# Early products of an output projection one block later, its late heads ahead of the last transposes, and two blocks' splits held behind evacuations

## The chip, the cores and the metric

The kernel runs on one core of a Trainium2 chip. The metric is the device time of one execution in microseconds. The core has a matrix engine (TensorE, PE in the profile), a vector engine (VectorE, DVE), a scalar engine (ScalarE, ACT), GpSimd (POOL) and SyncE (SP), whose queue issues most of the DMA transfers. Each engine takes its instructions in the order in which they stand for it, and waits on semaphores for the others.

## The reference, cut to what matters

Two layers over 1024 tokens of width 1024. The first mixes tokens by latent attention, the second by differential attention; each mixer and each feed-forward is followed by a normalisation of the sum with its input. The change lies at the end of the second layer's mixer:

```python
def block(args):                       # one block of 128 queries
    logits = einsum('bqhmd,bkhmd->bmhqk', q_b, k) * scale - slopes * dist   # two maps m per head
    logits = where(chunk_mask, logits, NEG_BIG)
    p = softmax(logits)
    a = p[:, 0] - lam * p[:, 1]
    return einsum('bhqk,bkhe->bqhe', a, v)
...
o = _rmsnorm(o, g_sub) * (1.0 - lambda_init)     # per head
mix = o.reshape(b, s, 8 * 128) @ w_o
h = _layernorm(ALPHA * h + mix, ...)
h = _layernorm(ALPHA * h + (silu(gate) * up) @ w_down, ...)
```

There are 8 heads of width 128 and 8 blocks of 128 queries; block i sees keys 0 to 128 (i + 1).

## The kernel before

All products are kept to float32 accuracy by splitting each operand into a high and a low part in float32r: ScalarE casts the high part, VectorE (or GpSimd) subtracts it for the low one, and three products, high by high, high by low and low by high, are added in PSUM.

**Attention of the second layer.** `attention` goes through the 64 pairs of head and block, head by head; the last head takes its blocks in the order 6, 7, 4, 5, 2, 3, 0, 1. For each pair there are three steps. `score` (two pairs ahead) makes the scores of both maps in PSUM, VectorE adds the bias and takes the maximum (L231), ScalarE exponentiates and sums (L234), VectorE takes the reciprocal (L236), GpSimd scales the second map (L1306) and VectorE joins the two (L1307). `turn` transposes the probabilities on TensorE into PSUM (L160, tiles `pt`), and ScalarE (L255, `pth`) and VectorE (L256, `ptl`) evacuate their high and low parts. `mix`, once for two blocks, multiplies them by the values (L267, tile `o`), and VectorE copies the result into `bo` (L1316). Per head the rows are then normalised: squares on ScalarE (L1331), a sum over partitions on TensorE (L1337, `ms`), logarithm and exponential on ScalarE (L1340, L1342), and a product on GpSimd (L1343). Heads 0 to 5 are stored to DRAM; heads 6 and 7 stay in `bo`.

**Output projection.** `OutProj` loads its weights, already split, by SP's queue as soon as the input activations are no longer needed (L358, tiles `wo`; `who` and `wlo` for heads 6 and 7, L363), and reads back heads 0 to 5 of a query block (`of`, L371). The table in the caller puts its steps in between the last head's pairs: after pair `b + slot` (b = 54) `early` multiplies some of heads 0 to 5 of the first block (6) or the second (7); `late` splits heads 6 and 7 of a block, multiplies them and adds the result to the residual (L414, with a sum for the normalisation). `rest` then does the remaining blocks whole, 4, 5, 2, 3, 0, 1: `of` loads and splits heads 0 to 5 (L394 on ScalarE, L395 on VectorE), `late` the other two, and `layer_norm` (L178 to L196) and `raw_x` (transposes `xTp`) follow. After it comes the feed-forward.

**What sets the order.** The program is written in this order, but the framework reorders it: it lays the instructions on a modelled timeline, by when their operands are ready there and by their priority, and each engine's list comes out of that. `high_priority` raises a step; `behind(i, j)` keeps instruction i after j. The PSUM banks in this stage are 3 for scores and sums (`s`), 2 for `m`, 2 for transposes (`t`) and 1 for `o`. `newest["hi"]` and `newest["lo"]` name the last `pth` and `ptl` evacuations written so far.

## Time and profile before

| | |
|---|---|
| time, median of 3 runs | 2294.41 us (2293.27 to 2299.95) |
| profiled execution, its own time | 2294.99 us |
| its span in the trace | 2293.2 us, mean TensorE clock 0.996 |
| busy: PE, DVE, ACT, POOL | 2251.4, 1560.4, 1018.6, 877.9 us |
| last head of the attention with the early products | about 1500 to 1564 us |
| rest of the output projection | about 1564 to 1640 us |
| second feed-forward | from 1640 us to the end |

The rows of the trace quoted below name an engine, a line, an operation and a tile. In rows of the timeline the first number is the start in microseconds from the beginning of the span, the second the duration; brackets give the idle time just before, and what ended it. A mean of TensorE's granted clock stands in each window's row, 1.00 being full. Matmuls are pipelined: their durations overlap, so their cost on a full engine is the distance between starts.

### The profile page before, as it was taken

To read this page: it belongs to the slowest core of one execution; us is meant where nothing else is said; L and a number is where in the kernel's file an instruction comes from. 1 tells how busy PE (TensorE), PEld (TensorE's weight loads), DVE (VectorE), ACT (ScalarE), POOL (GpSimd) and SP (SyncE) were. 2 spreads that over 40 slices of the span, in tenths; PEclk is the share of its full clock that TensorE was granted. 3 is DMA by queue.
4 is the path that set the end of the run, shared out by engine and by line. 5 is a ranking of instruction groups with operands and counts; after the bars stand their busy time and mean duration, and the time that the engine had idled before them with its cause. 6 is when DMAs were issued, how large, how long until landed. Compare 5 with 4: busy or idle time off the path is not lost. (4 is left out here: it accounts for less than half of the span.)

```text
span 2293.2 us, 31159 instructions
## 1 busy us (share of the span) xinstructions
PE 2251.4 (98%) x11426; PEld 1918.7 (84%) x11426; DVE 1560.4 (68%) x2887; ACT 1018.6 (44%) x2101; POOL 877.9 (38%) x682
## 2 busy tenths in 40 slices
PE   9999999999999999999999999999999999999997
PEld 9888998888888887888888898977778888887886
DVE  6666665596656558777476766676587566658877
ACT  4465664342332324345455655555442233324353
POOL 2233451124444445555332424211024444436564
PEclk9999999999999999999999999999999999999999
DMA  5121335334323237544311202143344232337453
GB/s 205 41 94 61 117 99 190 142 139 144 108 87 120 93 116 305 200 176 166 104 45 33 69 25 70 38 193 120 124 166 155 70 128 80 127 126 301 144 203 123
DMA packets 104281, 289.33 MB, mean 126 GB/s; under 512 B 8640, under 2 KB 31808, under 8 KB 93632
## 3 DMA queue, kind: packets, MB, share of 16 engines
q1 hardware_dynamic: 100128, 277.90, 34.5%
q0 software_dynamic: 4000, 9.44, 1.4%
q8 instruction: 90, 1.47, 0.3%
q14 instruction: 63, 0.52, 0.1%
HBM read 205.78 MB, written 77.33 MB: 123 GB/s over the span
## 5 line engine op out<-in xcount | busy, mean ns | idle before, releaser
L486 ACT CAST op_g<-gr 128x512 fp32r<-128x512 f32 x240 | 147.5, 622 | 410.8 <-PE gb L531 229.9
L487 POOL TENSOR_TENSOR op_g<-gr,op_g 128x512 fp32r<-128x512 f32 x104 | 145.3, 1402 | 304.1 <-DVE tmp L622 154.0
L487 DVE TENSOR_TENSOR op_h<-rh,op_h 128x512 fp32r<-128x512 f32 x154 | 166.4, 1112 | 68.1 <-ACT op_h L486 68.1
L531 PE MATMUL ga<-xh_m,op_g 128*128 128x512 f32 x512 | 168.1, 389 | 0.0
L486 ACT CAST op_h<-rh 128x512 fp32r<-128x512 f32 x154 | 92.6, 619 | 148.7 <-DMA rh<-h_dr 39.9
L799 PE MATMUL dw<-op_w_t,op_h 128*128 128x512 f32 x660 | 151.5, 390 | 0.3 <-DVE op_h L487 0.3
L799 PEld LDWEIGHTS dw<-op_w_t,op_h 128*128 128x128 f32 x660 | 123.5, 188 | 26.4 <-DVE op_h L487 1.0
L234 ACT ACTIVATE l_b<-l_b,mx_b 128x256 f32<-128x256 f32 (+7 forms) x128 | 99.5, 778 | 75.9 <-DVE mx_b L231 74.0
L1306 POOL TENSOR_SCALAR l_b<-l_b,r_b,cst 128x128 f32<-128x128 f32 (+3 forms) x64 | 52.5, 821 | 207.6 <-DVE r_b L236 201.6
L487 POOL TENSOR_TENSOR op_w_t<-tt,op_w_t 128x512 fp32r<-128x512 f32 x66 | 100.1, 1521 | 80.0 <-ACT op_w_t L486 77.6
L799 PE MATMUL dx<-op_w_b,op_h 128*128 128x512 f32 x528 | 123.5, 394 | 5.4 <-ACT op_w_b L486 3.9
L799 PEld LDWEIGHTS dx<-op_w_b,op_h 128*128 128x128 f32 x528 | 99.8, 190 | 28.7 <-ACT op_w_b L486 4.7
L531 PE MATMUL gb<-t4h_f,op_g 128*128 128x512 f32 x352 | 115.9, 390 | 3.0 <-DVE tmp L614 3.0
L531 PE MATMUL gc<-b22h_f,op_g 128*128 128x512 f32 x352 | 115.6, 389 | 2.3 <-ACT op_g L486 2.3
L531 PE MATMUL gc<-t1h_f,op_g 128*128 128x512 f32 x352 | 115.5, 389 | 0.0
L487 DVE TENSOR_TENSOR op_g<-gr,op_g 128x512 fp32r<-128x512 f32 x136 | 109.5, 806 | 8.8 <-ACT op_g L486 8.2
L531 PE MATMUL gb<-t3h_f,op_g 128*128 128x512 f32 x352 | 115.2, 389 | 0.0
L531 PE MATMUL gb<-t2h_f,op_g 128*128 128x512 f32 x352 | 114.9, 389 | 0.0
L531 PEld LDWEIGHTS ga<-xh_m,op_g 128*128 128x128 f32 x512 | 96.1, 188 | 19.9
L487 POOL TENSOR_TENSOR op_g<-s,op_g 128x512 fp32r<-128x512 f32 x40 | 55.5, 1387 | 144.0 <-ACT op_g L486 144.0
L155 PE MATMUL bp<-xT_f,h_wb 128*128 128x512 f32 x256 | 102.8, 402 | 0.0
L157 PE MATMUL bp<-xT_f,l_wb 128*128 128x512 f32 x256 | 101.6, 397 | 0.0
(373 smaller groups left out, 6767.7 us busy)
## 6 DMA issues: line engine op xcount, KB each, us to landing
gr<-in_w_gu SPq DMA_DIRECT2D x44, 1024.0 KB, 6.8
rh<-h_dr SPq DMA_DIRECT2D x28, 1024.0 KB, 5.2
h_dr<-sh SPq DMA_DIRECT2D x22, 1024.0 KB, 4.9
h_dr<-hp SPq DMA_DIRECT2D x22, 768.0 KB, 4.1
tt<-in_w_dn SPq DMA_DIRECT2D x22, 512.0 KB, 7.6
rh<-h_dr SPq DMA_DIRECT2D x14, 768.0 KB, 4.4
z<-xs_dr SPq DMA_DIRECT2D x16, 512.0 KB, 11.1
rw_b<-in_w_dn SPq DMA_DIRECT2D x8, 1024.0 KB, 8.2
```

The costliest lines, as they stand in the source:

```text
L155: T.matmul(ps_out, lh, rh, start=(i == 0), stop=False)
L157: T.matmul(ps_out, ll, rh, start=False, stop=(i == n - 1))
L234: newest["exp"] = A.activation(l[:, :n], l[:, :n], AF.Exp, bias=mx, scale=-1.0, accum_out=sm).ins
L486: A.copy(hi, src)
L487: eng.tensor_tensor(lo, src, f32(hi), ALU.subtract)
L531: T.matmul(o, w[:, a, kc], x[b][:, k, :], start=(first and k == 0 and (a, b) == (0, 0)), stop=(k == 3 and a == 1), skip_group_check=True,)
L799: T.matmul(o, h[:, a, c], w[:, b_], start=(first and (a, b_) == (0, 0)), stop=(last and a == 1), skip_group_check=True,)
L1306: G.tensor_scalar(l1[:, :n], l1[:, :n], r1, nlam, ALU.mult, ALU.mult)
```

## The change

Three things are edited. The five `early` steps of the table move by one slot, so each is written one pair later; the `late` step of block 6 moves from slot 9 to slot 8, so it is written ahead of the transposes of the last pair instead of behind them; and in `split`, for blocks 4 and 5 and for the piece that begins at head 0, both halves are kept behind the newest `pth` and `ptl` evacuations, which at that point are the last ones of the attention.

```diff
         def split(self, tb, hs, o):
             oh, ol = (t[:, hs] for t in self.oh[tb])
-            A.activation(oh, o, AF.Copy, scale=self.scale)
-            V.scalar_tensor_tensor(ol, o, self.scale, f32(oh), ALU.mult, ALU.subtract)
+            i = A.activation(oh, o, AF.Copy, scale=self.scale)
+            j = V.scalar_tensor_tensor(ol, o, self.scale, f32(oh), ALU.mult, ALU.subtract)
+            if tb in LAST_ORDER[2:4] and hs.start == 0:
+                behind(i.ins, newest["hi"])
+                behind(j.ins, newest["lo"])
...
         for slot, what, args in (
-            (2, "early", (first, (0, 1))), (3, "early", (first, (2, 3))), (4, "early", (first, (4, 5))),
-            (6, "early", (second, (0, 1, 2))), (7, "early", (second, (3, 4, 5))),
-            (9, "late", (first,)),
+            (3, "early", (first, (0, 1))), (4, "early", (first, (2, 3))), (5, "early", (first, (4, 5))),
+            (7, "early", (second, (0, 1, 2))), (8, "early", (second, (3, 4, 5))),
+            (8, "late", (first,)),
         ):
```

Lines behind the edit stand three further down in the changed kernel (L406 becomes L409, L1307 becomes L1310). In the names below `b7_3_0` is head 7, block 3, the first map or quarter; `a1_6` is block 6 of this projection; the long number at the end is a counter.

The first early product on TensorE, before:

```order
L228 MATMUL s_b7_6_1_1_15075<-bk1_10190,bq1_10188 128x448
L228 MATMUL s_b7_6_1_1_15075<-bk1_10190,ql1_10193 128x448
L406 MATMUL zp_a1_6_0_0_15285<-wo1_0_15132,oh_a1_6_15117 128x512 x2
L406 MATMUL zp_a1_6_1_0_15292<-wo1_0_15132,oh_a1_6_15117 128x512 x2
L228 MATMUL s_b7_7_0_0_15153<-bk1_10190,bq1_10188 128x512
```

and in the changed kernel:

```order
L228 MATMUL s_b7_6_1_1_15075<-bk1_10190,bq1_10188 128x448
L228 MATMUL s_b7_6_1_1_15075<-bk1_10190,ql1_10193 128x448
L409 MATMUL zp_a1_6_0_0_15338<-wo1_0_15132,oh_a1_6_15117 128x512 x2
L409 MATMUL zp_a1_6_1_0_15345<-wo1_0_15132,oh_a1_6_15117 128x512 x2
L228 MATMUL s_b7_7_0_0_15153<-bk1_10190,bq1_10188 128x512
```

Nothing moved here but the counters: the product stands behind the same scores. All five engines' lists, and what each row in them waits for, are the same up to the end of the last head.

There VectorE's rows begin to differ. Before, from the low part of block 2's second pair on:

```order
L256 TENSOR_TENSOR ptl_b7_2_1_15549<-pt_b7_2_0_15540,pth_b7_2_1_15548 128x128
L395 SCALAR_TENSOR_TENSOR oh_a1_4_15773<-of_a1_4_15771,cst_63,oh_a1_4_15773 128x768
L395 SCALAR_TENSOR_TENSOR oh_a1_5_15864<-of_a1_5_15862,cst_63,oh_a1_5_15864 128x768
L236 RECIPROCAL r_b7_0_1_15536<-sm_b7_0_1_15534 128x1
...
L256 TENSOR_TENSOR ptl_b7_2_0_15545<-pt_b7_3_0_15596,pth_b7_2_0_15544 128x2x128
L1307 SCALAR_TENSOR_TENSOR l_b7_0_0_15518<-l_b7_0_0_15518,r_b7_0_0_15526,l_b7_0_1_15528 128x128
...
L414 SCALAR_TENSOR_TENSOR z_a1_6_15121,sum_a1_6_15123<-z_a1_6_15121,zp_a1_6_0_6_15657 128x512
L414 SCALAR_TENSOR_TENSOR z_a1_6_15121,sum_a1_6_15123<-z_a1_6_15121,zp_a1_6_1_6_15665 128x512
L1316 COPY bo_10191<-o_b7_1_15630 128x256
L395 SCALAR_TENSOR_TENSOR oh_a1_4_15773<-bo_10191,cst_63,oh_a1_4_15773 128x256
L1307 SCALAR_TENSOR_TENSOR l_b7_1_0_15574<-l_b7_1_0_15574,r_b7_1_0_15582,l_b7_1_1_15584 128x256
```

and in the changed kernel, from the same row on:

```order
L256 TENSOR_TENSOR ptl_b7_2_1_15549<-pt_b7_2_0_15540,pth_b7_2_1_15548 128x128
L236 RECIPROCAL r_b7_0_1_15536<-sm_b7_0_1_15534 128x1
...
L1310 SCALAR_TENSOR_TENSOR l_b7_0_0_15518<-l_b7_0_0_15518,r_b7_0_0_15526,l_b7_0_1_15528 128x128
...
L417 SCALAR_TENSOR_TENSOR z_a1_6_15121,sum_a1_6_15123<-z_a1_6_15121,zp_a1_6_0_6_15652 128x512
L417 SCALAR_TENSOR_TENSOR z_a1_6_15121,sum_a1_6_15123<-z_a1_6_15121,zp_a1_6_1_6_15660 128x512
L256 TENSOR_TENSOR ptl_b7_2_0_15545<-pt_b7_3_0_15576,pth_b7_2_0_15544 128x2x128
L1310 SCALAR_TENSOR_TENSOR l_b7_1_0_15554<-l_b7_1_0_15554,r_b7_1_0_15562,l_b7_1_1_15564 128x256
L256 TENSOR_TENSOR ptl_b7_0_0_15627<-pt_b7_0_0_15624,pth_b7_0_0_15626 128x128
...
L256 TENSOR_TENSOR ptl_b7_0_0_15627<-pt_b7_1_0_15668,pth_b7_0_0_15626 128x2x128
L395 SCALAR_TENSOR_TENSOR oh_a1_4_15773<-of_a1_4_15771,cst_63,oh_a1_4_15773 128x768
```

The two wide splits (768 columns) have gone behind the last low part; the low part of block 3's first pair (`ptl_b7_2_0` from `pt_b7_3_0`) has gone from before both joinings to behind the two additions of block 6. On ScalarE the two wide splits go behind the last `pth` cast in the same way, and the exponentials of blocks 0 and 1 stand ahead of the casts of block 3.

TensorE's rows at that place, before:

```order
L160 MATMUL pt_b7_0_0_15644<-ident_61,l_b7_0_0_15518 128x128
L267 MATMUL o_b7_1_15630<-pth_b7_2_1_15548,bvh3_2_14411 128x256
...
L160 MATMUL pt_b7_1_0_15650<-ident_61,l_b7_1_0_15574 128x128 x2
...
L267 MATMUL o_b7_0_15673<-pth_b7_0_0_15646,bvh3_0_13933 128x256
L267 MATMUL o_b7_0_15673<-ptl_b7_0_0_15647,bvh3_0_13933 128x256
...
L406 MATMUL zp_a1_7_1_6_15734<-who1_7_15148,oh_a1_7_15126 128x512
L406 MATMUL zp_a1_4_0_0_15781<-wo1_0_15132,oh_a1_4_15773 128x512 x3
```

and in the changed kernel:

```order
L267 MATMUL o_b7_1_15610<-pth_b7_2_1_15548,bvh3_2_14411 128x256
L160 MATMUL pt_b7_1_0_15668<-ident_61,l_b7_1_0_15554 128x128 x2
...
L267 MATMUL o_b7_0_15673<-pth_b7_0_0_15626,bvh3_0_13933 128x256
L409 MATMUL zp_a1_4_0_0_15781<-wo1_0_15132,oh_a1_4_15773 128x512 x2
L267 MATMUL o_b7_0_15673<-ptl_b7_0_0_15627,bvh3_0_13933 128x256
...
L409 MATMUL zp_a1_7_1_6_15734<-who1_7_15148,oh_a1_7_15126 128x512
L409 MATMUL zp_a1_5_0_0_15872<-wo1_0_15132,oh_a1_5_15864 128x512 x2
L409 MATMUL zp_a1_4_0_0_15781<-wo1_0_15132,oh_a1_4_15773 128x512
```

The transposes of the last block (1) stand five products earlier, and the first products of blocks 4 and 5 are mixed in; the late products of block 6 keep their place, ahead of all of these.

## The prediction

> **What bounds the kernel now.** I read the page first, then the waits of TensorE (PE) around the change, then the same stretch by windows, and last the engines' rows in order of time.

> ```profile
> PE 2251.4 (98%) x11426; PEld 1918.7 (84%) x11426; DVE 1560.4 (68%) x2887; ACT 1018.6 (44%) x2101; POOL 877.9 (38%) x682
> ```

> PE is busy for 2251.4 of 2293.2 us and the change removes no product, so all that can be won anywhere is 41.8 us of idle PE plus what a lowered clock costs. Between 1480 and 1700 us the waits that matter are (us in total, times, longest):

> ```profile
> PE zp_a L406 <- DMA wo<-wo_dr: 3.7, 1, 3.7
> PE pt_b L160 <- DVE l_b L1307: 2.2, 1, 2.2
> ```

> The first is the first early product waiting for the output weights, the other the last block's transposes waiting for its probabilities. Each lowers the clock too (column PEclk, the one before the DMA share):

> ```profile
> 1508.00:1510.00 2.00, 0.00 (x0) 0.00 (x0) 2.00 (x6) 1.14 (x2) 0.00 (x0) 0.67 1.07 412
> 1510.00:1512.00 2.00, 1.62 (x4) 1.36 (x5) 1.74 (x7) 0.27 (x1) 0.00 (x0) 0.50 0.96 383
> 1512.00:1514.00 2.00, 2.00 (x6) 1.41 (x6) 0.00 (x0) 0.00 (x0) 0.00 (x0) 0.50 1.03 430
> 1514.00:1516.00 2.00, 2.00 (x11) 1.67 (x10) 0.43 (x1) 0.98 (x2) 0.00 (x0) 0.63 0.98 406
> 1558.00:1560.00 2.00, 0.60 (x4) 0.59 (x5) 1.90 (x8) 0.15 (x1) 0.00 (x0) 0.97 0.00 0
> 1560.00:1562.00 2.00, 2.00 (x6) 1.54 (x5) 0.76 (x2) 1.63 (x5) 0.00 (x0) 0.50 0.01 4
> 1562.00:1564.00 2.00, 2.00 (x11) 1.85 (x10) 1.65 (x4) 0.12 (x1) 0.56 (x1) 0.68 0.04 8
> ```

> At the second place the clock is halved for 0.06 + 2 / 1 + 1.28 us, about 3.4 us in all, which loses 1.7 us. At the first it is halved for about 6.8 us, of which PE works some 5.1 and loses 2.6.

> **The change part by part.** *Early products one block later.* Nothing moves: PE's rows, and every other engine's, stand as before up to the last transposes, the first early product still behind the same scores. Its wait stays:

> ```profile
> 1506.35 0.36 PE L228 MATMUL s_b<-bk,ql 128*128 128x448 f32 x1
> 1510.38 2.05 PE L406 MATMUL zp_a<-wo,oh_a 128*128 128x512 f32 x4 [3.67 <-DMA wo<-wo_dr]
> ```

> SP's queue is unchanged there as well, so the weights land when they did. This part counts 0; 3.7 + 2.6 = 6.3 us would be its price if it worked, and that end belongs to a rival.

> *Splits of blocks 4 and 5 behind the last evacuations.* This is where the time is. VectorE (DVE) before:

> ```profile
> 1551.53 0.08 DVE L231 DVE_READ_ACCUMULATOR2_ANT mx_b<- 128x1 f32 x1
> 1552.07 1.93 DVE L395 SCALAR_TENSOR_TENSOR oh_a<-of_a,cst,oh_a 128x768 fp32r<-128x768 f32 x2
> 1553.92 0.15 DVE L236 RECIPROCAL r_b<-sm_b 128x1 f32<-128x1 f32 x1
> 1554.48 0.42 DVE L256 TENSOR_TENSOR ptl_b<-pt_b,pth_b 128x256 fp32r<-128x256 f32 x1
> 1556.84 0.67 DVE L414 SCALAR_TENSOR_TENSOR z_a<-z_a,zp_a 128x512 f32<-128x512 f32 x1
> 1558.38 0.48 DVE L395 SCALAR_TENSOR_TENSOR oh_a<-bo,cst,oh_a 128x256 fp32r<-128x256 f32 x1
> 1558.78 0.48 DVE L1307 SCALAR_TENSOR_TENSOR l_b<-l_b,r_b,l_b 128x256 f32<-128x256 f32 x1
> 1561.67 1.28 DVE L188 SCALAR_TENSOR_TENSOR z_a<-z_a,nmu_a,gb 128x1024 f32<-128x1024 f32 x1 [0.99 <-ACT zp_a L182]
> ```

> and ScalarE (ACT) and GpSimd (POOL):

> ```profile
> 1550.79 1.76 ACT L394 ACTIVATE oh_a<-of_a,cst 128x768 fp32r<-128x768 f32 x2 [0.25 <-PE s_b L228]
> 1552.46 0.39 ACT L234 ACTIVATE l_b<-l_b,mx_b 128x128 f32<-128x128 f32 x1
> 1556.13 0.51 ACT L234 ACTIVATE l_b<-l_b,mx_b 128x256 f32<-128x256 f32 x1
> 1560.11 0.70 ACT L182 ACTIVATE zp_a<-z_a,nmu_a 128x512 f32<-128x512 f32 x1
> 1554.24 0.45 POOL L1306 TENSOR_SCALAR l_b<-l_b,r_b,cst 128x128 f32<-128x128 f32 x1 [4.23 <-DVE r_b L236]
> 1557.10 0.55 POOL L1306 TENSOR_SCALAR l_b<-l_b,r_b,cst 128x256 f32<-128x256 f32 x1 [0.24 <-DVE r_b L236]
> ```

> I walk the new order with these durations, 0.1 to 0.2 us for a change of engine, on the old clock. The maximum of block 0's second map is there at 1551.6, and ACT, freed of its 1.76 us, exponentiates by 1552.2. The reciprocal ends at 1552.4 (before 1554.07). Scores of block 1's first map go to 1552.8; POOL and L1307 finish block 0 by 1553.4; ACT's exponential ends at 1553.5, the second map at 1554.1, its exponential at 1554.8, its reciprocal at 1554.95, POOL at 1555.7.

> *Late heads ahead of the last transposes.* On PE they keep their place; on DVE their two additions (L414, 1.3 us together) now stand ahead of the low half of block 3's first pair, and run 1554.95 to 1556.25. That low half ends at 1556.65 (before 1554.90), L1307 of block 1 at 1557.1 (before 1559.26). So the wait for L1307 ends 2.1 us earlier, and a new one stands ahead of it. PE before:

> ```profile
> 1554.96 0.39 PE L267 MATMUL o_b<-ptl_b,bvh 128*128 128x256 f32 x1
> 1555.18 0.28 PE L267 MATMUL o_b<-pth_b,bvl 128*128 128x256 f32 x1
> 1555.30 0.28 PE L267 MATMUL o_b<-pth_b,bvh 128*128 128x256 f32 x1
> 1559.40 0.41 PE L160 MATMUL pt_b<-ident,l_b 128*128 128x128 f32 x2 [2.22 <-DVE l_b L1307]
> 1564.46 0.39 PE L406 MATMUL zp_a<-who,oh_a 128*128 128x512 f32 x1
> 1564.69 3.81 PE L406 MATMUL zp_a<-wo,oh_a 128*128 128x512 f32 x16
> ```

> In the new order PE waits for that low half until 1556.7 instead of 1554.96; the second pair's high half, which ACT copies only behind it, is there at 1557.1; block 1's transposes run at 1557.4, behind the low half of block 0 that DVE clears after L1307; the second pair's low half, behind the two means, comes at 1557.95. Five products at 0.12 us (starts 1555.18 and 1555.30) end at 1558.6, six of block 7's late ones at 0.23 us (1564.46 to 1564.69) at 1560.0. Then a third wait: ACT runs the two squares (L182, 1.5 us) before the copy of block 1's transposes (1559.5) and the held split of block 4 (0.9 us, 1560.4); DVE copies the group's output at 1559.1 and, since L188 (1.2 us) is ahead, gives block 0's low half at 1561.0. Five products and block 7's other six end at 1563.0 instead of 1564.69, and two products of block 4 (0.46 us) are already done, so the same work is reached 1.69 + 0.46, about 2.2 us earlier, if the clock stays full.

> The clock is the unknown. From one side, a longer gap later left it alone: starts 0.33, then 0.24 us apart behind it.

> ```profile
> 1670.09 0.50 PE L531 MATMUL gc<-b22h_f,op_g 128*128 128x512 f32 x1 [2.33 <-ACT op_g L486]
> 1670.42 0.40 PE L531 MATMUL gc<-b22l_f,op_g 128*128 128x512 f32 x1
> 1670.66 0.42 PE L531 MATMUL ga<-xh_m,op_gp 128*128 128x512 f32 x1
> ```

> From the other, the 2.22 us gap did halve it. In the new order PE idles 0.7 us before 1555.15 (ACT copies block 3's first pair only behind the exponentials), 1.4 us to 1556.7 and 0.4 us to 1558.0: some 2.4 us within 3.4, hardly less than before (PE busy for 0.60 of the two microseconds ahead of 1560). So I take one halved stretch of 3.4 us again, 1.7 us; of it the waits ahead of 1558.0, 1560.4 and 1561.0, 0.4 + 0.4 + 0.1 us, hide about 0.8, since PE comes later to them. The gain is 2.2 - 0.9 = 1.3 us. Ends: no stretch halved, 2.2; two halved and nothing hidden, 2.2 - 3.4 = -1.2, a loss.

> [...]

> *What else moves.* The held splits (3.7 us of ACT and DVE) now run at about 1559.5 to 1563.6, beside products of blocks 7 and 4; without that cover PE would wait their length, and block 4's copy is already in the sum. They release the buffers for the next loads of heads 0 to 5, so SP issues those about 10 us later:

> ```profile
> 1553.10 1.29 SPq L371 DMA_DIRECT2D of_a<-o_dr  x2
> 1590.37 4.98 PE L406 MATMUL zp_a<-wo,oh_a 128*128 128x512 f32 x20 [0.15 <-ACT oh_a L394]
> 1571.00 0.34 SPq L546 DMA_DIRECT2D gp<-in_w_gu  x1
> 1640.47 0.48 PE L531 MATMUL ga<-xh_m,op_gp 128*128 128x512 f32 x1
> ```

> Block 2 uses them at 1590.37, some 25 us on. The first feed-forward weights now queue behind the second normalised block's store; they are used at 1640.47, and that cover is over 60 us. The other difference, products of block 5 begun before block 4's second half, exchanges equal products. In the last feed-forward a few casts change places beside a busy PE: nothing.

> **The rivals.** (1) *The clock stays full* behind the tail, as behind the 2.33 us gap: 2.2 us, 2292.2. For it: no single piece of idle is over 1.4 us. Against: they lie close together. [...] (2) *The label works*: the weight wait goes, 6.3 us, with the tail's 1.3 us 2286.8. For it speaks the change's name; against it that PE's rows are the same. (3) *The gain is taken back* at 1667 us, where PE waits 2.33 us for ACT while DVE has no idle time:

> ```profile
> 1660.00:1680.00 20.00, 17.66 (x79) 14.20 (x78) 20.00 (x34) 13.27 (x25) 0.00 (x0) 1.00 0.36 132
> ```

> If that stage were paced by loads rather than by PE's last projection, the wait would grow by what PE gains: 2294.4. Against it: its inputs start from the last normalised block, which moves with PE. (4) *Slower*: the low half behind the two additions starves PE so that two stretches are halved, +1.2 us, and if the 2.33 us gap then halves one too, 1.7 more: 2295.6 to 2297.3. It decides once PE works over 4.4 us at half speed behind the tail, which loses the 2.2 us. For it: more pieces of idle than before. Against: each is shorter.

> **How the numbers follow.** The profiled execution took 2294.99 us around its span of 2293.2, 0.6 above the median 2294.41 of 2293.27 to 2299.95; 1.3 us off the median gives 2293.1. Chances: forecast 0.42 (with rival 1 its own range is 2291.5 to 2294), full clock 0.28, taken back 0.12, slower 0.10, the label working 0.03, and 0.05 for a scatter as wide as the three runs'. The range 2289 to 2298 takes in the ends of the unknown, each widened by 1 to 2 us, as the lower two runs lie 1.1 apart; it leaves out the label and the scatter. A measurement of this kernel tells about 0.3% (6.9 us) from no change. Below 2287.5 lie rival 2 and 0.01 of the scatter, 0.04; above 2301.3 the rest of the scatter, 0.04; between them 0.92.

> **What would show it.** Right: the wait for the output weights still near 3.7 us; the wait for L1307 gone or small, with new waits for the low half (L256) summing to some 2 to 3 us between 1554 and 1562; block 4's long run of products at about 1562 to 1563 on the old clock; the distance from there to the end unchanged. Wrong: no weight wait, a clock halved for over 3.4 us behind 1556, or a longer wait at 1667.

## The result, and the profile after

| | before | changed |
|---|---|---|
| median of 21 runs each | 2296.16 us | 2291.98 us |
| lowest, highest | 2291.92, 2299.95 | 2288.91, 2295.44 |
| ratio, 95% interval | | 0.9986, 0.998 to 0.9992 |
| profiled execution, span | 2294.99, 2293.2 us | 2293.0, 2291.2 us |

The change takes 1.8 to 4.6 us off, 3.2 us by the ratio. That is within the 0.3% taken as no change, and the time lies inside the predicted range, 1.1 us below the predicted 2293.1. The gain is larger than the forecast 1.3 us, and the parts of the sum behave differently from how they were put.

The page's busy times of the changed kernel:

```profile
PE 2248.8 (98%) x11426; PEld 1915.5 (84%) x11426; DVE 1558.3 (68%) x2887; ACT 1018.7 (44%) x2101; POOL 875.9 (38%) x682
```

The waits of TensorE between 1480 and 1700 us (total, times, longest):

```profile
PE zp_a L409 <- DMA wo<-wo_dr: 4.7, 1, 4.7
PE gc L534 <- ACT op_g L489: 2.1, 1, 2.1
PE o_b L267 <- DVE ptl_b L256: 1.1, 1, 1.1
```

The wait for L1307 (now L1310) is gone, and two shorter ones stand in its place: 1.1 us for L256 and, in the rows below, 0.37 us for L255. The wait for the weights is still there. TensorE's rows in order of time, of the changed kernel:

```profile
1510.51 2.05 PE L409 MATMUL zp_a<-wo,oh_a 128*128 128x512 f32 x4 [4.70 <-DMA wo<-wo_dr]
...
1552.76 0.60 PE L160 MATMUL pt_b<-ident,l_b 128*128 128x128 f32 x4
...
1554.27 0.39 PE L267 MATMUL o_b<-pth_b,bvh 128*128 128x256 f32 x1 [0.37 <-ACT pth_b L255]
1555.75 0.38 PE L267 MATMUL o_b<-ptl_b,bvh 128*128 128x256 f32 x1 [1.09 <-DVE ptl_b L256]
...
1556.57 0.39 PE L160 MATMUL pt_b<-ident,l_b 128*128 128x128 f32 x2
...
1562.02 4.26 PE L409 MATMUL zp_a<-wo,oh_a 128*128 128x512 f32 x18
...
1637.37 0.48 PE L534 MATMUL ga<-xh_m,op_gp 128*128 128x512 f32 x1
```

and the row of the kernel before that answers to the second of these, the transposes of block 3:

```profile
1553.44 0.60 PE L160 MATMUL pt_b<-ident,l_b 128*128 128x128 f32 x4
```

Up to these transposes TensorE's two instruction lists are the same, and the 0.68 us between them are a difference of executions. So they serve as the mark from which the last stage is measured, and the first feed-forward product (1640.47 before, 1637.37 now) as its end: 87.03 us before, 84.61 us after. This stage became 2.42 us shorter. The long run of block 4's products comes 9.26 us behind the mark instead of 11.25, and two of its products (0.46 us) are already done by then: 2.45 us, so all of the gain is made before that run begins.

The clock, from the windows of the changed kernel (the number before the DMA share):

```profile
1510.00:1512.00 2.00, 1.49 (x4) 1.23 (x5) 0.84 (x4) 0.00 (x0) 0.00 (x0) 0.50 1.02 395
1512.00:1514.00 2.00, 2.00 (x9) 1.57 (x8) 0.00 (x0) 0.00 (x0) 0.00 (x0) 0.65 0.99 418
...
1554.00:1556.00 2.00, 0.63 (x3) 0.44 (x4) 2.00 (x7) 1.34 (x5) 1.28 (x2) 1.00 0.00 0
1556.00:1558.00 2.00, 1.96 (x15) 1.68 (x15) 1.51 (x7) 2.00 (x7) 0.00 (x0) 1.00 0.00 0
```

Behind the weight wait it is halved here too, for 3.4 us where the kernel before had 6.8; behind block 3's transposes it stays full, where the kernel before had 3.4 us of half speed.

### The profile page after: what moved, and what is told of

Read it like the earlier page. It is cut to its first block, busy times and chain, and to the rows that moved or that the text cites. A ratio compares the mean times of both kernels' runs of the same rounds, so it can differ in the third digit from the quotient of the medians.

```text
span 2291.2 us, 31161 instructions
## 1 busy us (share of the span) xinstructions
PE 2248.8 (98%) x11426; PEld 1915.5 (84%) x11426; DVE 1558.3 (68%) x2887; ACT 1018.7 (44%) x2101; POOL 875.9 (38%) x682
## 5 line engine op out<-in xcount | busy, mean ns | idle before, releaser
L490 DVE TENSOR_TENSOR op_h<-rh,op_h 128x512 fp32r<-128x512 f32 x154 | 158.3, 1060 | 71.0 <-ACT op_h L489 70.9
L234 ACT ACTIVATE l_b<-l_b,mx_b 128x256 f32<-128x256 f32 (+7 forms) x128 | 99.6, 778 | 78.1 <-DVE mx_b L231 76.2
```

The source lines that it names most:

```text
L234: newest["exp"] = A.activation(l[:, :n], l[:, :n], AF.Exp, bias=mx, scale=-1.0, accum_out=sm).ins
L490: eng.tensor_tensor(lo, src, f32(hi), ALU.subtract)
```

## The experiments

Two distances are used below. The *last stage* is the one just described, from block 3's transposes to the first feed-forward product. The *stretch before it* runs from the start of block 6's last score (448 columns) to block 3's transposes: 1506.35 to 1553.44, 47.09 us in the kernel before.

The theory after the comparison is that only the hold on the splits acts; it shortens the chain of maximum, exponential and joining; and part of what is won is the clock, which was halved before and is not now. The rivals are that the table's moves carry part of it, that the clock's part is hidden by later waits, and that the weight wait is worth its 6.3 us.

**1. The table's moves alone.**

```diff
-            if tb in LAST_ORDER[2:4] and hs.start == 0:
-                behind(i.ins, newest["hi"])
-                behind(j.ins, newest["lo"])
```

> Only the table's moves: the five early steps one slot later and the late step one slot earlier, without the hold on the splits. Theory (the table's moves reach no engine, all of the gain comes from the hold): ratio to the kernel before 1.000, within 0.0006; the wait for the output weights stays at 3.7 to 4.7 us, and the last block's transposes wait for L1307 for about 2.2 us as before. Rival (the early steps do what their label says): the weight wait goes, 3 to 6 us faster. Rival (the late step carries part of the gain): 1 to 2 us faster. [...]

Measured: ratio 0.9994 (0.9985 to 1.0003). The lists of all five engines are those of the kernel before. In this second profile of them:

```profile
1550.51 0.60 PE L160 MATMUL pt_b<-ident,l_b 128*128 128x128 f32 x4
...
1556.46 0.66 PE L160 MATMUL pt_b<-ident,l_b 128*128 128x128 f32 x2 [2.22 <-DVE l_b L1307]
...
1561.65 3.82 PE L406 MATMUL zp_a<-wo,oh_a 128*128 128x512 f32 x16
...
1637.41 0.48 PE L531 MATMUL ga<-xh_m,op_gp 128*128 128x512 f32 x1
```

The last stage takes 86.90 us, against 87.03: it repeats within 0.13 us, though the marks lie 2.9 us earlier. The wait for L1307 is 2.22 us again, that for the weights 3.08. So two of the three edits in the change's name reach no engine by themselves. The halved stretch is there too, 3.4 us long, but it begins 0.2 us ahead of the transposes that end the wait; in the first profile it began 0.5 us behind them.

**2. The hold on block 4's split alone.**

```diff
-            if tb in LAST_ORDER[2:4] and hs.start == 0:
+            if tb in LAST_ORDER[2:3] and hs.start == 0:
```

> The change with the hold on block 4's split alone, block 5's left free. Theory (block 5's split follows block 4's on both engines anyway, so one hold is the whole change): as the changed kernel, ratio 0.9986 (0.998 to 0.9992), 1.8 to 4.6 us faster than before; the wait for L1307 gone, the wait for the low half (L256) about 1.1 us, long run of products 9.3 us behind block 3's transposes. Rival (each hold is worth its own half of the 3.7 us of splits): about half, 0.9993. A second look at the changed kernel's lists: with the clock full in the tail again the full-clock sum (2.2 us) stands, with one halved stretch of 3.4 us the forecast's 1.3 us.

Measured: 0.9989 (0.9979 to 0.9998). The lists are those of the changed kernel, so one hold on one block does all that the two holds do; block 5's split follows by itself. This run has the table's moves too. No run has the holds without them, but the program built so has the changed kernel's lists on every engine, so the hold is the whole change. The last stage runs from 1553.72 to 1638.32, 84.60 us, with a full clock. The same kernel was timed once more at the end:

> The changed kernel's instruction lists once more (the hold on block 4's split alone, which gives the same lists), beside the run below on the same chip. If the change is worth the 2.36 us that its last stage shows, the ratio to the kernel before is 0.9990 within the 0.0008 that eleven runs leave open; if the 3.2 us of the first timing are the true value, 0.9986. [...]

Measured: 0.9991 (0.9982 to 0.9999); last stage 1553.79 to 1638.36, 84.57 us, clock full again. Three profiles give 84.61, 84.60 and 84.57 us, two of the kernel before's lists 87.03 and 86.90: the last stage is 2.4 us shorter. Three timings of these lists give 3.2, 2.5 and 2.1 us, and the intervals of all three hold the 2.4.

**3. The hold on block 5's split alone.**

```diff
-            if tb in LAST_ORDER[2:4] and hs.start == 0:
+            if tb in LAST_ORDER[3:4] and hs.start == 0:
```

> The change with the hold on block 5's split alone: block 4's (0.9 us on ScalarE, 1.0 us on VectorE) stays inside the softmax chain, and 18 of block 4's first products (0.23 us each, 4.1 us) come to stand ahead of the last pair's products on TensorE. Theory A (the softmax chain of blocks 0 and 1 sets the end of the tail): L1307 of block 1 comes about 1 us later than in the changed kernel, so about 1 us of the gain is lost, ratio 0.999. Theory B (TensorE's waits behind the last transposes set it): the products cover the waits for block 0's copies (0.4 + 0.1 us and what follows), ratio 0.9984 or lower, at least as fast as the changed kernel.

```profile
1552.77 0.60 PE L160 MATMUL pt_b<-ident,l_b 128*128 128x128 f32 x4
...
1559.02 4.26 PE L409 MATMUL zp_a<-wo,oh_a 128*128 128x512 f32 x18
...
1636.93 0.48 PE L534 MATMUL ga<-xh_m,op_gp 128*128 128x512 f32 x1
```

Measured: 0.9992 (0.9984 to 1.0001), which lies nearer theory A's number and by its interval decides nothing; the last stage takes 84.16 us, 0.4 less than in the changed kernel. Block 1's transposes come 4.61 us behind the mark (3.81 in the changed kernel), but 18 products of block 4 run in the shadow of what follows. Theory B holds for the stage: the joining may come later, if TensorE has products to put behind it.

**4. The halved clock: the gap of the kernel before, covered.** TensorE gets matmuls on a constant, which nothing reads, behind the last product of blocks 2 and 3; all waits for data stay.

```diff
+        def cover():
+            t = ps_s("cover")
+            for i in range(20):
+                behind(T.matmul(t[:, :P], ones, ones, start=True, stop=True).ins, newest["mix"])
+
+        at(8 * H - 2, cover)
```

> The kernel before, with 20 matmuls of 128 x 128 on a constant (0.11 us each at full clock, nothing reads them) behind the last product of blocks 2 and 3, so that TensorE stays busy for about 2.3 us of the 2.22 us that it waited for L1307; every wait for data stays. 18 of block 4's products also come to stand ahead of block 0's. Measured by the distance from block 3's transposes (four L160 at 1553.44 in the kernel before) to the first feed-forward product, which took 87.03 and 86.90 us in two profiles of the kernel before's lists. [...] Rival (the halving belongs to the wait for data or costs little, because later waits hide it): a halved stretch again, or a distance of 86.5 to 87 us.

Measured: no halved stretch between 1550 and 1570 us, but each matmul shows as two, 40 in all, and they lasted 4.68 us: block 1's transposes came 8.08 us behind the mark instead of 5.96, and the last stage took 87.57 us. The clock's part could not be read from that. With half as many:

> As the run before of that name, but with half as many matmuls on the constant: in the trace each of them had shown as two of 0.117 us, so that 20 lasted 4.7 us and delayed block 1's transposes by 2.1 us. 10 last 2.3 us, about the 2.22 us of the wait, and in TensorE's list up to the end of block 4's first products nothing else changes. Theory (the halved stretch behind the wait costs the kernel before its 1.7 us): no halved stretch between 1550 and 1570, the transposes at their old distance of 5.96 us from block 3's, and the distance to the first feed-forward product 85.2 to 85.5 us instead of 87.03 and 86.90. Rival (the halving is hidden by later waits, and all of the change's 2.36 us come from the earlier joining): 86.7 to 87.1 us.

```profile
1551.86 0.60 PE L160 MATMUL pt_b<-ident,l_b 128*128 128x128 f32 x4
...
1555.43 2.44 PE L1409 MATMUL cover<-ones 128*128 128x128 f32 x20
1557.81 0.41 PE L160 MATMUL pt_b<-ident,l_b 128*128 128x128 f32 x2
...
1561.54 4.26 PE L406 MATMUL zp_a<-wo,oh_a 128*128 128x512 f32 x18
...
1637.37 0.48 PE L531 MATMUL ga<-xh_m,op_gp 128*128 128x512 f32 x1
```

The transposes stand 5.95 us behind the mark, as before, and the clock stays full. The last stage takes 85.51 us: 1.46 us less than the mean 86.97, with no wait for data shortened. The difference is there at once: the long run of block 4's products begins 9.68 us behind the mark instead of the 11.14 us of experiment 1. Up to that run TensorE's list differs by the added matmuls alone; behind it some products change places. The 2.4 us of the change are thus 1.46 us of clock and about 0.9 us of work that comes earlier.

**5. The new wait for the low half.** Block 6's two additions are kept behind the joining of block 1:

```diff
+            if last and tb == LAST_ORDER[0]:
+                behind(k.ins, newest["joined"])
```

> The change, with the two additions of block 6 (L417, 1.3 us) kept behind the joining of block 1 (L1310), so that the low half of block 3's first pair no longer stands behind them. Distance from block 3's transposes to the first feed-forward product: 84.61 and 84.60 us in two profiles of the changed kernel's lists. Theory (the 1.1 us wait for L256 is on the path, as the forecast's walk has it): the wait falls to under 0.3 us and block 1's transposes come 0.5 to 1 us earlier; distance 83.6 to 84.2 us. Rival (a later wait takes its place: for the held split, or for block 0's low half): the wait for L256 is gone, others grow by as much, 84.5 to 84.9 us. Clock full in both.

```profile
1556.33 0.39 PE L267 MATMUL o_b<-ptl_b,bvh 128*128 128x256 f32 x1 [1.11 <-DVE ptl_b L256]
```

Block 1's transposes come 2.85 us behind the mark instead of 3.81, but the wait only moved to the second pair's low half, now behind the additions: 1.11 us instead of 1.09. The last stage takes 84.38 us, 0.2 less. The rival has the mechanism right; the number lies between the two forecasts.

**6. The weight wait filled.** The first early products are kept behind the last scores of block 7 (`held` is the last score written at that point):

```diff
+                    if tb == LAST_ORDER[0] and h == 0 and a is oh and w == 0:
+                        behind(k.ins, newest["held"])
```

> The change, and the first early products (heads 0 and 1 of block 6) kept behind the last scores of block 7, so that in TensorE's list the scores, transposes and about 20 products of blocks 6 and 7 of the attention now stand ahead of the first product that needs the output weights. Theory (the label's price is real: weight wait 4.7 us and about 1 us lost to the halved clock behind it): the wait for the weights gone or under 1 us; TensorE has about 4.6 us of work to put there, but VectorE is busy until 1510.8 us, so new waits of 1 to 2 us on scores or copies; 3 to 5 us faster than the changed kernel, ratio to the kernel before 0.9965 to 0.9975. Rival (VectorE's chain holds TensorE there anyway): the wait is only renamed, as the changed kernel, 0.9986. Rival (the tail lengthens, because the products taken from the start are then missing as cover later): 0.999 to 1.000.

```profile
1508.08 0.37 PE L228 MATMUL s_b<-bk,ql 128*128 128x448 f32 x1
1510.50 0.50 PE L228 MATMUL s_b<-bk,bq 128*128 128x512 f32 x1 [2.05 <-DVE mx_b L231]
...
1553.63 0.60 PE L160 MATMUL pt_b<-ident,l_b 128*128 128x128 f32 x4
```

Measured: 0.9991 (0.9982 to 1.0), no faster than the changed kernel. The wait for the weights is gone, and one of 2.05 us for a score bank that VectorE must clear has taken its place, with one of 0.62 us behind it; the clock is halved there too, for 3.4 us. The stretch before the last stage takes 45.55 us, against 47.32, 46.41 and 48.74 us in the changed kernel's three profiles, and the last stage 85.23, 0.6 more. Six further profiles in which TensorE's list is the same up to block 3's transposes, two of them of the lists before, took 45.71 to 48.10 us for that stretch, so 45.55 us is hardly a gain. Most of the 3 to 5 us was not to be had. Next, block 7's read-back and split were issued behind the weight loads, so that VectorE has one split less to do there:

```diff
-            for tb in LAST_ORDER[:2]:
-                self.of(tb)
+            self.of(LAST_ORDER[0])
...
                     self.wo.append(t)
+            self.of(LAST_ORDER[1])
```

> The change, with the first early products kept behind the last scores of block 7 as in the run before, and block 7's read-back and its split (0.9 us on ScalarE, 1.0 us on VectorE) issued behind the weight loads. Distance from the last score of block 6 (second 448 columns of the second map) to block 3's transposes: 45.55 us with the products held alone, 46.41 and 47.32 us in two profiles of the changed kernel. Theory (the weight wait turned into a wait for VectorE, whose list had two splits in it there): the 2.05 us wait for a score bank falls by about 1 us, distance 44 to 44.8 us. Rival (the score chain itself, maximum, exponential and join, sets that place): the waits stay near 2.7 us and the distance near 45.5 us.

```profile
1505.80 0.36 PE L228 MATMUL s_b<-bk,ql 128*128 128x448 f32 x1
...
1550.25 0.60 PE L160 MATMUL pt_b<-ident,l_b 128*128 128x128 f32 x4
```

```profile
PE pt_b L160 <- DVE ptl_b L256: 1.9, 1, 1.9
...
PE s_b L228 <- DVE mx_b L231: 0.2, 1, 0.2
```

The wait for the score bank falls to 0.2 us, and one of 1.9 us for a low half appears. The stretch takes 44.45 us, as the theory had it, though the waits did not go as it said: their sum fell only from 2.7 to 2.1 us.

**7. The pieces together.** With the additions late as in 5:

> The change with three further edits together: the first early products behind block 7's last scores, block 7's read-back behind the weight loads, and block 6's two additions behind block 1's joining. Theory (the pieces add): from the last score of block 6 to the first feed-forward product 129.2 to 129.7 us, against 134.1 and 132.8 in two profiles of the kernel before and 131.9 and 131.0 of the changed kernel; 4 to 4.5 us faster than the kernel before, ratio 0.998 to 0.9984, about 1.5 us faster than the changed kernel. Rival (what is won there is given back at the feed-forward's wait near 1665 us, which lasted 2.0 to 2.5 us in every profile, or by the clock): as the changed kernel, 0.9986 to 0.999.

```profile
PE ga L538 <- DVE op_gp L494: 3.7, 1, 3.7
```

From block 6's last score to the first feed-forward product it took 128.84 us, the least of all, and yet the ratio is 0.9988 (0.9979 to 0.9996). The scheduler had also moved subtractions on VectorE in the feed-forward: its wait, which ends at 1665.07 us, is now 3.7 us long, and the clock is halved for 6.8 us there. The trace bears out the rival; the interval of the ratio alone does not part it from the theory. With the hold on block 5 alone instead of the late additions:

> The first two of these edits, with the hold on block 5's split alone, so that block 4's first products can cover the waits behind the last transposes. Theory (as with the hold on block 5 alone, where the distance from block 3's transposes to the first feed-forward product was 84.16 us instead of 84.6): about 0.4 us below the run with the two edits (129.69 us from the last score of block 6), 129.2 to 129.6 us, ratio 0.998 to 0.9984. Rival: the changed kernel's 0.9986 to 0.999.

Measured: 0.9978 (0.9969 to 0.9987), 129.49 us. And once more, beside the changed kernel:

> The fastest of the kernels so far once more, beside the changed kernel on the same chip. Theory (from block 6's last score to the feed-forward it is 1.5 to 2.4 us shorter than the changed kernel): 1.5 to 2.4 us below the run above, ratio to the kernel before 0.9978 to 0.9984. Rival (the first timing was a lucky draw, and what is won is given back at the feed-forward's wait near 1665 us): as the run above.

Measured: 0.9987 (0.9978 to 0.9996), 130.83 us; median 2291.88 us beside 2291.93 of the changed kernel. So it is faster than the kernel before in both timings, and whether it beats the changed kernel stays open: once it lay lower, once not. These two profiles, however, show the clock's price a second time. Of the first:

```profile
1549.31 0.60 PE L160 MATMUL pt_b<-ident,l_b 128*128 128x128 f32 x4
...
1554.68 0.41 PE L160 MATMUL pt_b<-ident,l_b 128*128 128x128 f32 x2 [1.78 <-DVE l_b L1312]
...
1634.27 0.48 PE L536 MATMUL ga<-xh_m,op_gp 128*128 128x512 f32 x1
```

and of the second:

```profile
1549.72 0.60 PE L160 MATMUL pt_b<-ident,l_b 128*128 128x128 f32 x4
...
1555.09 0.41 PE L160 MATMUL pt_b<-ident,l_b 128*128 128x128 f32 x2 [1.77 <-DVE l_b L1312]
...
1636.19 0.48 PE L536 MATMUL ga<-xh_m,op_gp 128*128 128x512 f32 x1
```

The same lists and the same wait, 1.78 and 1.77 us, but 84.96 and 86.47 us to the feed-forward. The windows from 1550 to 1570 us show why, first profile, then second:

```profile
1550.00:1570.00 20.00, 18.12 (x89) 14.30 (x88) 16.47 (x37) 11.30 (x28) 3.75 (x6) 1.00 0.35 115
```

```profile
1550.00:1570.00 20.00, 18.13 (x83) 14.35 (x82) 15.07 (x39) 10.54 (x26) 4.11 (x6) 0.91 0.27 79
```

A mean of 0.91 over 20 us is one stretch of 3.4 us at half speed; it came in one execution and not in the other, and cost 1.51 us.

## Why the prediction was right, and where not

**Early products, 0: right.** Experiment 1 has the lists and the last stage of the kernel before. The weight wait stayed, but not at 3.7 us: 3.07 to 5.37 us in three profiles of the changed kernel, 3.08 to 3.67 in two of the kernel before. It is a wait for a transfer, and in the changed kernel's three profiles it was longer where TensorE arrived earlier: 5.37, 4.70 and 3.07 us where block 6's last score began at 1505.05, 1505.44 and 1507.31.

**Its price of 6.3 us, and rival 2: too high.** With the wait filled and block 7's split moved, the stretch before the last stage took 44.45 us. That is 3.0 us less than the mean of 47.49 in the changed kernel's three profiles, and 2.4 us less than the mean of 46.83 over the nine profiles in which TensorE's list is the same up to block 3's transposes; the last stage gave 0.6 us back. The rest was not there, because VectorE, busy with splits and the maxima, stops TensorE at that place anyway (2.05 us with the wait alone filled). The 0.03 for that rival rightly rested on the lists; its size was the sum of a wait and its clock, without asking what is late next.

**Splits out of the softmax chain: right.** The wait for L1307 went as said. On VectorE and ScalarE of the changed kernel:

```profile
1555.28 0.42 DVE L256 TENSOR_TENSOR ptl_b<-pt_b,pth_b 128x256 fp32r<-128x256 f32 x1
1555.62 0.54 DVE L1310 SCALAR_TENSOR_TENSOR l_b<-l_b,r_b,l_b 128x256 f32<-128x256 f32 x1
...
1559.47 0.41 DVE L256 TENSOR_TENSOR ptl_b<-pt_b,pth_b 128x256 fp32r<-128x256 f32 x1
```

```profile
1558.20 1.76 ACT L394 ACTIVATE oh_a<-of_a,cst 128x768 fp32r<-128x768 f32 x2
```

With the 0.68 us between the executions taken off, the walk put the end of the low half's wait at 1556.02 (measured 1555.75), block 1's transposes at 1556.72 (1556.57), the second pair's low half at 1557.27 (1556.99), block 0's low half at 1560.32 (ends 1559.88) and the long run at 1562.32 (1562.02). It is 0.15 to 0.44 us too late throughout. What the attribution got wrong is the name: the exchange on VectorE was listed under the late heads, but by experiment 1 it does not occur without the hold. The walk's gain of 2.2 us was measured as 2.45.

**The clock, minus 0.9: the step that failed.** The walk took some 2.4 us of idle TensorE within 3.4 us and so a halved stretch again. The trace has 0.37 and 1.09 us there. The third wait, for the held split and block 0's low half, all but vanished:

```profile
1559.19 0.73 PE L409 MATMUL zp_a<-wo,oh_a 128*128 128x512 f32 x2
1559.94 0.39 PE L267 MATMUL o_b<-ptl_b,bvh 128*128 128x256 f32 x1
```

The first two products that need the split began at 1559.19, where the walk had it ready at 1559.72, and they cost 0.75 us instead of the usual 0.46. No stretch was halved in three profiles of these lists. That was rival 1, which had a chance of 0.28. That its 2292.2 us are 0.2 from the median is chance: the forecast started from the median of three runs, 2294.41, and the 21 runs beside the changed kernel have 2296.16. The gain of 1.3 us lies outside the 1.8 to 4.6 us of the first timing, and 2.2 inside, while the intervals of the two later timings hold both; the predicted range held because it was wide enough for a full clock and a halved one alike. The price of a halved stretch was also put too high, 1.7 us where 1.46 to 1.56 were measured. (Its length was read rightly as 3.4 us, though the first term of that sum should be 0.12 us, not 0.06.) The 2.2 us of rival 1, too, are not what they were taken for: they are measured against a kernel whose clock had been halved. At a full clock on both sides the change is worth about 0.9 us (85.51 against 84.59); the other 1.46 us are the halved stretch that went. How often it comes no run shows: both profiles of the lists before have it, none of the three of the changed kernel's, and one of the two profiles of equal lists in experiment 7. So the change is worth an estimated 0.9 us where neither side's clock is halved there and 0.9 + 1.46, about 2.4 us, where only the kernel before's is.

**Rivals 3 and 4: no.** The wait at 1667 us was 2.10 us in this profile and 2.5 and 2.7 us in the other two, against 2.33 and 2.2; the way from the feed-forward's first product to the products just ahead of that wait stayed 26.9 to 27.0 us in all five. The clock was halved behind it in the three changed profiles and not in the two before, so the second part of rival 4 did occur. What a halved stretch costs can be read there a third time. In the changed kernel 14 products took 4.89 us from the end of the wait:

```profile
1666.83 0.65 PE L534 MATMUL gc<-b22h_f,op_g 128*128 128x512 f32 x1 [2.10 <-ACT op_g L489]
...
1671.72 0.39 PE L534 MATMUL gc<-t1h_f,op_g 128*128 128x512 f32 x1
```

In the kernel before they took 3.33 us, from 1670.09 to the row

```profile
1673.42 0.39 PE L531 MATMUL gc<-t1h_f,op_g 128*128 128x512 f32 x1
```

which makes 1.56 us. As the kernel before with its first gap covered twice, 20 and 10 matmuls, showed it once halved and once not, nothing here ties that to the change.

**The noise around it.** Up to block 6's last score TensorE's lists in the kernels above are the same, and yet that score begins between 1503.81 and 1508.08 us. By their spans (2293.2 and 2292.9 us before, 2291.2, 2292.4 and 2293.5 us changed) single profiles would have shown anything from 0.6 us lost to 2.0 us won; the length of the last stage repeats to 0.13 us. Other stages do not: the stretch before it took 45.71 to 48.74 us in nine profiles with the same list on TensorE, with most of the spread in the weight wait of 3.07 to 5.37 us, and from the feed-forward's first product to the end it is 652.8 and 655.5 us in two profiles of the lists before, 653.9 to 655.1 in three of the changed kernel. So that the rest stays unchanged, as forecast, is shown only to some 3 us.

## What to carry to other kernels

Compare the order that the engines really get before pricing a table's moves: here two of three edits reached no engine by themselves, and one hold on one split was the whole change. Where a wait is shortened, ask separately for its length and for the clock behind it; here a wait of 2.22 us cost 1.46 us more in the work that followed, and two waits of 0.37 and 1.09 us with work between them left the clock full, which won more than their lengths show. Measure a change of 0.1% as the distance between two marks inside one profile, across several profiles, beside the timings, and see first how far that distance repeats.

## What the runs showed of the hardware

Edges of the halved clock, in windows of 0.2 us, of the kernel before (a mean of 0.68 puts the edge 0.07 us behind the window's start):

```profile
1508.60:1508.80 0.20, 0.00 (x0) 0.00 (x0) 0.20 (x3) 0.06 (x1) 0.00 (x0) 0.68 1.00 410
...
1559.80:1560.00 0.20, 0.20 (x3) 0.16 (x2) 0.10 (x1) 0.15 (x1) 0.00 (x0) 0.68 0.00 0
```

and of the changed kernel:

```profile
1510.00:1510.20 0.20, 0.00 (x0) 0.00 (x0) 0.20 (x3) 0.00 (x0) 0.00 (x0) 0.51 1.06 389
1667.00:1667.20 0.20, 0.20 (x1) 0.18 (x2) 0.20 (x1) 0.20 (x2) 0.00 (x0) 0.54 1.06 451
```

The share of the last 3.41 us ahead in which TensorE was busy goes with this. Ahead of the tail's halved stretch in the kernel before it is 0.35, and at about the same place in the changed kernel, a whole number of 3.41 us from its halved stretches and with a full clock behind it, 0.67 (busy time of PE is the second number):

```profile
1556.51:1559.92 3.41, 1.19 (x9) 1.03 (x10) 3.18 (x12) 1.20 (x5) 0.91 (x2) 0.99 0.23 70
```

```profile
1554.37:1557.79 3.42, 2.29 (x15) 1.85 (x16) 2.96 (x11) 2.75 (x8) 1.17 (x2) 1.00 0.00 0
```

In the 14 profiles, between 1495 and 1690 us and counted in steps of 3.41 us from each profile's own halved stretches, a halved step followed all 22 full-clock steps with the lowest shares, 0.00 to 0.45, and none of the 14 with 0.60 to 0.75; of the six from 0.46 to 0.57 it followed two. The two profiles of equal lists in experiment 7 are among these six, 0.53 (full) and 0.46 (halved). So the share as the profile shows it does not settle every case, and three profiles with a full clock do not show that the changed kernel's always stays full. The length of a single gap settles it less: a halved stretch came with gaps of 1.77 and 2.22 us, and the clock stayed full behind 1.78 us in experiment 7 and behind 2.33 us in the kernel before.

The wait for the weights took up the difference between two executions of the changed kernel's lists: it was 3.07 us where block 6's last score began at 1507.31 and 5.37 us where it began at 1505.05, and its end lay at 1510.73 and 1510.79.
